# A hybrid decoder step on one core: other numbers in the guess that orders the program

## The chip, the cores and the metric

The kernel runs on one core of a Trainium2 chip. The metric is the device time of one execution in microseconds (us), as the median of several runs. Engines are named as in the profile: PE is TensorE, DVE is VectorE, ACT is ScalarE, POOL is GpSimd, SP is the engine that issues most DMAs.

## The reference

One layer of a causal decoder is computed for a prompt of 2048 tokens and for 8 x 4 sample tokens, all in fp32:

```python
def decoder_layer(x, mk, mv, s5_re, s5_im, ret_s, pos0, p):
    h = rmsnorm(x, p['g_mix'])
    proj = h @ p['w_in']              # columns: u, q, k, v, g
    ...
    ssm_out, s5_re_new, s5_im_new = s5_mixer(...)      # B u, scan over time, C x + D u, gelu, glu
    ret_out, ret_new = retention_mixer(q, k, v, g, ret_s, pos0, p['ret_gn'])  # 4 heads, chunks of 128
    x = x + jnp.concatenate([ssm_out, ret_out], axis=-1) @ p['w_out']
    x = x + memory_attend(rmsnorm(x, p['g_xattn']), mk, mv, p['w_mq'], p['w_mo'])
    h = rmsnorm(x, p['g_mlp'])
    x = x + jnp.square(jax.nn.relu(h @ p['w_up'])) @ p['w_down']
    return x, s5_re_new, s5_im_new, ret_new
```

The width is 1024, the S5 mixer has 512 channels with a complex state, the retention 4 heads of 128, the memory 256 tokens, the MLP 4096 columns. A last RMSNorm follows.

## The kernel before

The prompt is cut into four blocks of 512 tokens (block 1 also carries the 32 sample tokens). Every large product is made of three matmul passes over a high and a low part of each operand. A weight unit of 128x1024 is loaded as `raw`, its high part is taken on ACT and its low part (`whl<-raw,whl`) on DVE as one instruction or on POOL as four.

The program has two halves. The mixer half goes through the blocks: v projection, then for each of the four heads q, k and g, then the u projection of the block; in front of the u projection of blocks 1 to 3 stand the two `w_glu` units of the block before (`dn<-z,whl`, those of block 3 come later). The memory keys and values follow. The second half goes through the blocks again: attention over the memory, MLP, final norm.

The order of all instructions is made when the program is built, and is fixed then. `Order.run` writes the main line: the big matmuls (`dn`, `sc`, `zps`, `tms`), in a sequence that no number changes. Beside it run side chains, generators such as `retention` (one per head and block: `pkd`, `psc`, then `pkv`, then `po`, then `pt`), `ret_sample` (`px`, `po2`, `pn`, `pt2`, which the listings show as `po` and `pt` too), `s5_setup` (`qt`, `km`), `s5_batch` (four per block: `pu`, `vr` and `vi`, then the scan on DVE, then `py`, `pf`, in the sample block also `pvs`, `pys`, `pfs`) and `s5_gelu`. A side chain gives up control at each `yield`, and `Order.poll` resumes it when `od.clock` has come to its wake time. That time is a guess: `Model` keeps when each engine will be free and when each tile is ready, from a fixed and a per-element time for each engine (`RATE`), and adds an offset in ns from the hand-tuned table `SET` (`"sb4": 700`, `"re5": 550`). `od.clock` itself goes on by the guessed time of each matmul (`mm`, `tr`). `Model` also decides which of DVE and POOL takes an operation whose key in `SET` is 2.

At some places the main line may not go on without a chain. `Order.join` then resumes side chains until that chain is done, and writes all that they still have to do into the program before the next main matmul:

```python
def join(self, s):
    self.until(lambda: s.done)

def until(self, cond):
    while not cond():
        self.resume(min(self.sides, key=lambda x: x.wake))
```

The mixer half has four such places that matter here: the end of block 0, where `s5_setup` must be done, and the `w_glu` units of blocks 0, 1 and 2, which stand at the end of the heads of blocks 1, 2 and 3 and wait for the whole S5 chain of the block before, the gelu of its fourth batch included. They are called join 1 to join 4 below. At run time each engine takes its own instructions strictly in the written order and waits on semaphores for the others.

Of the kernel before, what the change touches and what calls it, by code (L numbers as in the profile page):

```python
# [15 lines left out]
PSUM = bass.MemoryType.PSUM  # L16
# [43 lines left out]
class Item:  # L60


    def __init__(self, fn, src=None, eng=None, side=None, cond=None, tight=False, tag="lo"):
        self.fn, self.src, self.eng, self.side, self.cond, self.tight = fn, src, eng, side, cond, tight
        self.raw = self.hl = self.lo = self.again = self.into = None
        self.tag = tag
        self.keep = False
# [7 lines left out]
class Model:  # L75


    RATE = {"V": (65.0, 1.042), "A": (80.0, 0.834), "G": (140.0, 2.11)}

    def __init__(self):  # L80
        self.free = dict(V=0.0, A=0.0, G=0.0, SP=0.0, DMA=0.0)
        self.bufs, self.rings, self.last, self.table = {}, {}, 0.0, None

    def name(self, tile, ring, bufs):
        self.bufs[tile.name] = dict(w={}, r={}, prev=None, ring=(self.rings.setdefault(ring, []), bufs))
        return tile
# [75 lines left out]
    def done(self, eng, name, outs, ins, func=None):  # L162
        n = 1
        for d in max((ap.shape for ap in outs + ins), key=lambda x: len(x) and np.prod(x[1:]))[1:]:
            n *= d
        if name == "dma_start":
            t = self.free["SP"] = max(self.free["SP"] + 60.0, self.after("DMA", outs, ins) - 1200.0)
            t = max(t + 1200.0, self.free["DMA"])
            end = t + 91.0 + 4.0 * n * outs[0].shape[0] / 360.0
            self.free["DMA"] = end  # L170
            self.note("DMA", outs, ins, end)
            return
        c, r = self.RATE[eng]
        end = max(self.free[eng], self.after(eng, outs, ins)) + c + r * n
        if func in (AF.Tanh, AF.Sin, AF.Exp) and func != self.table:
            self.table = func
            end += 1280.0
        self.free[eng] = end
        self.last = max(self.last, end)
        self.note(eng, outs, ins, end)  # L180
# [20 lines left out]
class Either:  # L201
# [5 lines left out]
    def __getattr__(self, name):  # L207
        def call(*args, **kw):
            i = SET[self.key]
            if i == 2:  # L210
# [4 lines left out]
                for e in self.engines:  # L215
                    c, r = Model.RATE[e.key]
                    when.append(max(self.model.free[e.key], self.model.after(e.key, [out], ins, True)) + c + r * n)
# [111 lines left out]
def tile_decoder_step(ctx: ExitStack, tc: tile.TileContext, ins: dict, outs: dict):  # L329
    nc = tc.nc  # L330
    model = Model()
    V, A, G, SY = (Engine(model, e, k) for e, k in ((nc.vector, "V"), (nc.scalar, "A"), (nc.gpsimd, "G"), (nc.sync, "SP")))
# [90 lines left out]
    def split_unit(raw, eng, pool=None, tag="whl", bufs=NW):  # L423
# [4 lines left out]
        def lo():  # L428
            e = eng or min((V, G), key=lambda e: max(model.free[e.key], model.ready(hl)) + 1024 * Model.RATE[e.key][1])
            n = 256 if e is G else 1024  # L430
            for i in range(0, 1024, n):
                e.tensor_tensor(out=hl[:, 1, i:i + n], in0=raw[:, i:i + n], in1=hl[:, 0, i:i + n].bitcast(F32), op=ALU.subtract)
        return hl, lo

    od = Order(model, load_unit, split_unit)

    def mm(out, lhsT, rhs, start, stop):
        n = 1
        for d in rhs.shape[1:]:
            n *= d  # L440
        m = lhsT.shape[1]
        if lhsT.dtype == F32R:
            c = max(0.4217 * n, 107.0 if m > 64 else 56.0)
        else:
            c = max(1.69 * n, 214.0)
        od.work(out, [lhsT, rhs], c)
        T.matmul(out, lhsT, rhs, start=start, stop=stop)  # L447

    def tr(out, in_, idn):
        od.work(out, [in_, idn], 109.0)  # L450
        T.transpose(out, in_, idn)  # L451

    def split_first(dst, src, scale=None):
# [31 lines left out]
    def fm(w, acts, t, out, nk=KT, order=None):  # L485

        for o, n in pieces(t) if isinstance(t, int) else t:
            out.append((dense(), o, n))
        for j, k in enumerate(order or range(nk)):
            for i, (a, b) in enumerate(PASSES):  # L490
                for ps, o, n in out:
                    mm(ps[:, :n], w(k, a), acts[k][:, b, o:o + n],
                       start=(j == 0 and i == 0), stop=(j == nk - 1 and i == 2))
            if j < nk - 1:
                yield

    def stats(pool, acc, cols, eps_tag):

        n = len(cols)
        st = aux("st")  # L500
        ms = pool.tile([P, n], F32, tag=eps_tag + "ms", name="ms")
        full = [i for i, c in enumerate(cols) if c[1] == P]
        part = [i for i, c in enumerate(cols) if c[1] < P]
        for i, (sl, r, *rest) in enumerate(cols):
            for j, s in enumerate([sl] + rest):
                mm(st[:r, 2 * i:2 * i + 2], s, ones, start=(j == 0), stop=(j == len(rest)))
        if part:
            V.memset(ms, 1.0)
        nf = len(full)
        V.tensor_scalar(ms[:, :nf], st[:, 0:2 * nf:2], 1.0 / D, EPS, op0=ALU.mult, op1=ALU.add)  # L510
        for i in part:
            r = cols[i][1]
            V.tensor_scalar(ms[:r, i:i + 1], st[:r, 2 * i:2 * i + 1], 1.0 / D, EPS, op0=ALU.mult, op1=ALU.add)
        return rsqrt(pool, eps_tag, ms, n)
# [5 lines left out]
    def spread(dst, rs, t, last=None, row=None):  # L520

        nt = min(t, BT) // P
        b = aux("sp")
        if row is not None:
            W = [8, 4, P]
            parts = com.tile([P, 2, 4], F32R, tag="parts", name="parts")
            V.tensor_copy(parts[:, 0], rs[:, :4])
            V.tensor_tensor(out=parts[:, 1], in0=rs[:, :4], in1=parts[:, 0].bitcast(F32), op=ALU.subtract)
            yield "sa1"
            tr(b[:8, :P], parts.bitcast(F32).rearrange("p a b -> p (a b)"), ident)  # L530
            r = row[:8, :BT].bitcast(F32R)
            V.tensor_tensor(out=r.rearrange("p (a b) -> p a b", a=4), in0=b[:8, :P].unsqueeze(1).to_broadcast(W),
                            in1=pick.unsqueeze(2).to_broadcast(W), op=ALU.mult)
            yield "sa2"
            mm(b, ones_r.to_broadcast([8, P]), r, start=True, stop=True)
        else:
            for i in range(nt):
                mm(b[:, i * P:(i + 1) * P], rs[:, i:i + 1].to_broadcast([P, P]), ident, start=True, stop=True)
        A.activation(dst[:, :nt * P], b[:, :nt * P], AF.Copy)
        if t > BT:  # L540
            b2 = aux("sp2")
            mm(b2[:, :NS], rs[:NS, last:last + 1].to_broadcast([NS, P]), ident[:NS, :NS], start=True, stop=True)
            A.activation(dst[:, BT:BT + NS], b2[:, :NS], AF.Copy)
        return b
# [338 lines left out]
    def fm_item(src, view, acts, t, done, nk=KT, eng=None, order=None, tag="lo"):  # L883

        def fn(hl):
            for i, w in enumerate(view(hl)):
                out = []
                yield from fm(w, acts() if callable(acts) else acts, t, out, nk, order)
                done(i, out)
                yield  # L890
        return Item(fn, src, eng, tag=tag)
# [47 lines left out]
    def mem_items():  # L939
# [10 lines left out]
        def kv(which, o):  # L950
            def done(i, out):
                ps = out[0][0]

                def ev():
                    od.join(M["ld"])
                    sg = mk((P, TM_), "wst")[:, :MEM]
                    V.tensor_tensor(out=sg, in0=ps[:, :MEM], in1=M["rb"], op=ALU.mult)
                    SY.dma_start(outs[f"m{which}T"][o], sg)
                    t = mk((P, 2, MEM), f"{which}t").bitcast(F32R)
                    split_first(t, sg)  # L960
                    split_rest(t, sg)
                    T_[which].append(t)
                M.setdefault("ev", []).append(ev)
                if which == "v" or o:
                    for e in M["ev"]:
                        e()
                    M["ev"].clear()
            return fm_item(ins[f"w_m{which}"][o], one, acts, MEM, done, eng=ve(f"e_m{which}1" if o % 2 else f"e_m{which}"), tag="l_m" + which)
# [274 lines left out]
    def s5_chain(B):  # L1243
# [21 lines left out]
        def u4_of(be):  # L1265
            pu = aux2("pu")
            for j in range(4):
                tr(pu[:, j * P:(j + 1) * P], uT[:, 4 * be + j].rearrange("p a b -> p (a b)"), ident)
            u4 = mb((P, 4, P), "u4", 2)
            A.activation(u4, pu.rearrange("p (a b) -> p a b", a=4), AF.Copy)  # L1270
            mats["u4"] = u4
            B["u_read"] = be == 3
# [1102 lines left out]
```

## Time and profile before

| what | value |
|---|---|
| time, median of 3 runs | 3056.98 us (3055.93 to 3063.95) |
| the profiled execution | 3057.99 us, its span 3055.8 us |
| PE busy | 2944.5 us, 96% |
| DVE busy | 1767.3 us, 58% |
| POOL busy | 1314.5 us, 43% |
| ACT busy | 1007.1 us, 33% |

The span is the time from the first to the last instruction; the rest of the execution's time lies around it. PE is the engine whose idle time counts. Blocks 0 to 3 of the mixer half lie between about 30 and 756 us of the span, the second half from 968 us on. Idle time of the other engines costs nothing by itself.

### The profile page before, as it was taken

Reading aid. Unit: us, or ns where it says so; the run is one execution under the profiler, and the core shown is the slowest. Engines: PE = TensorE matmul, PEld = TensorE weight load, DVE = VectorE, ACT = ScalarE, POOL = GpSimd, SP = SyncE. Lnnn points to the kernel's source line nnn. Section 1 sums busy time; section 2 is a strip of 40 time slices with the busy share of each in tenths; the row PEclk is TensorE's granted clock in tenths of the full one; section 3 lists DMA queues with packets and bytes.
Section 4 is the critical chain, followed back from the end, with each engine's and each line's share of the span. In section 5 each row is a group of like instructions: output and inputs, shape, how many; then the busy total and the mean of one; then the engine's idle time right before and its main releaser. Section 6 shows DMA issues by size and latency. Waiting matters only on the chain.

```text
span 3055.8 us, 43238 instructions
## 1 busy us (share of the span) xinstructions
PE 2944.5 (96%) x16676; PEld 2561.3 (84%) x16676; DVE 1767.3 (58%) x3088; ACT 1007.1 (33%) x1440; POOL 1314.5 (43%) x1463
## 2 busy tenths in 40 slices
PE   8898899998989999999999999999999999999998
PEld 6688788877987978888987888788999998978887
DVE  8968858779675654334465555556533444553334
ACT  4442232322454332223333333433322223432222
POOL 5534434344565153334534344462433326153334
PEclk9999999999999999999999999999999999999999
DMA  5453253342685222234324444542222233232222
GB/s 151 137 171 111 83 154 119 115 156 75 230 269 168 90 93 95 96 97 141 114 88 145 145 149 148 198 134 83 91 84 90 90 132 122 81 99 94 96 90 76
DMA packets 138957, 374.37 MB, mean 123 GB/s; under 512 B 18656, under 2 KB 39808, under 8 KB 138752
## 3 DMA queue, kind: packets, MB, share of 16 engines
q1 hardware_dynamic: 138176, 371.10, 37.3%
q8 instruction: 131, 2.15, 0.3%
q14 instruction: 74, 0.61, 0.1%
q10 hardware_dynamic: 576, 0.52, 0.1%
HBM read 334.17 MB, written 37.40 MB: 122 GB/s over the span
## 4 chain that ended last, share of the span: by engine, by line
PE 65%; DVE 1%; issue 0%; DMA 0%; ACT 0%; POOL 0%; POOLq 0%; SPq 0%; ACTq 0%; DVEq 0%
PE dn L447 57%; PE sc L447 6%; PE zps L447 1%; DVE rst L197 1%; PE ptp L451 0%; PE st L447 0%; DVE rsy L197 0%; DMA raw<-in_w_down 0%; DVE act L197 0%; PE sp L447 0%; POOL x L197 0%; DVE mx L197 0%; ACT x L197 0%; DVE stage L197 0%; DVE ms L197 0%
## 5 line engine op out<-in xcount | busy, mean ns | idle before, releaser
L447 PE MATMUL dn<-actl,whl 128*128 128x512 f32 (+2 forms) x4656 | 916.3, 356 | 2.2 <-DVE x L197 2.2
L447 PE MATMUL dn<-act,whl 128*128 128x512 f32 (+2 forms) x4704 | 913.3, 348 | 2.1 <-POOL whl L197 1.6
L197 POOL TENSOR_TENSOR whl<-raw,whl 128x256 fp32r<-128x256 f32 x896 | 692.7, 805 | 510.8 <-ACT whl L197 494.3
L447 PEld LDWEIGHTS dn<-actl,whl 128*128 128x128 f32 x4656 | 767.7, 188 | 130.5 <-ACT whl L197 1.9
L447 PEld LDWEIGHTS dn<-act,whl 128*128 128x128 f32 x4704 | 752.7, 189 | 110.8 <-issue 3.0
L197 ACT ACTIVATE whl<-raw 128x1024 fp32r<-128x1024 f32 (+1 forms) x505 | 523.2, 1046 | 650.7 <-PE dn L447 460.5
L197 DVE TENSOR_TENSOR x<-dn,x 128x512 f32<-128x512 f32 (+2 forms) x496 | 291.4, 606 | 430.7 <-PE dn L447 430.2
L197 DVE TENSOR_TENSOR whl<-raw,whl 128x1024 fp32r<-128x1024 f32 (+1 forms) x281 | 400.0, 1429 | 174.3 <-ACT whl L197 164.2
L447 PE MATMUL dn<-z,whl 128*128 128x512 f32 (+1 forms) x2160 | 435.1, 352 | 0.0
L447 PEld LDWEIGHTS dn<-z,whl 128*128 128x128 f32 x2160 | 353.4, 188 | 56.5 <-issue 1.1
L197 POOL TENSOR_TENSOR actl<-sq,actl 128x512 fp32r<-128x512 f32 (+1 forms) x128 | 171.2, 1338 | 455.0 <-DVE sq L197 445.4
L197 DVE SCALAR_TENSOR_TENSOR relu<-dn,rb 128x512 f32<-128x512 f32 (+1 forms) x160 | 91.6, 589 | 323.4 <-PE dn L447 316.0
L197 ACT ACTIVATE actl<-relu 128x512 fp32r<-128x512 f32 (+1 forms) x128 | 82.2, 642 | 512.5 <-DVE relu L197 512.5
L447 PE MATMUL dn<-whl,act 128*128 128x512 f32 x768 | 203.0, 413 | 11.6 <-ACT whl L197 6.3
L197 POOL TENSOR_TENSOR acc<-acc,relu 128x512 f32<-128x512 f32 (+2 forms) x77 | 107.4, 1394 | 237.1 <-ACT relu L197 235.0
L447 PEld LDWEIGHTS dn<-whl,act 128*128 128x128 f32 x768 | 168.0, 255 | 35.9 <-ACT whl L197 7.0
L197 DVE TENSOR_TENSOR sq<-relu 128x512 f32<-128x512 f32 (+1 forms) x128 | 91.6, 715 | 14.8 <-POOL actl L197 2.3
L447 PE MATMUL sc<-whl,act 128*128 128x256 f32 x576 | 80.3, 291 | 14.2 <-ACT p L197 9.4
L447 PEld LDWEIGHTS sc<-whl,act 128*128 128x128 f32 x576 | 75.1, 197 | 15.6 <-ACT p L197 10.0
L447 PE MATMUL sc<-whl,z 128*128 128x256 f32 x576 | 80.8, 291 | 0.0
L197 DVE SCALAR_TENSOR_TENSOR act<-x,small,act 128x512 fp32r<-128x512 f32 (+2 forms) x76 | 64.4, 854 | 28.2 <-ACT act L197 28.2
L197 ACT ACTIVATE act<-x,small 128x512 fp32r<-128x512 f32 (+2 forms) x76 | 53.0, 701 | 72.8 <-DVE x L197 52.9
(318 smaller groups left out, 2671.8 us busy)
## 6 DMA issues: line engine op xcount, KB each, us to landing
raw<-in_w_up SPq DMA_DIRECT2D x128, 512.0 KB, 3.5
raw<-in_w_down SPq DMA_DIRECT2D x128, 512.0 KB, 3.5
raw<-in_w_out SPq DMA_DIRECT2D x32, 512.0 KB, 3.5
raw<-wq_d SPq DMA_DIRECT2D x32, 512.0 KB, 3.5
raw<-wo_d SPq DMA_DIRECT2D x32, 512.0 KB, 3.5
x<-in_xT SPq DMA_DIRECT2D x48, 256.0 KB, 4.3
pm<-pm_d SPq DMA_DIRECT2D x16, 768.0 KB, 5.3
tab<-tab_d SPq DMA_DIRECT2D x16, 516.0 KB, 4.4
```

The lines of the kernel that those rows point to most:

```text
L197: return f(*args, **kw)
L447: T.matmul(out, lhsT, rhs, start=start, stop=stop)
```

## The change

The guess gets other numbers: larger fixed times for DVE, ACT and POOL instructions and slightly larger times per element, larger times for matmuls (230 instead of 216 ns for one of 512 columns), and a new rule: an instruction of DVE with two inputs that both lie in SBUF, if it would start within one of the last 64 POOL instructions, starts when that instruction ends. Nothing else is touched, the table `SET` neither.

```diff
-    RATE = {"V": (65.0, 1.042), "A": (80.0, 0.834), "G": (140.0, 2.11)}
+    RATE = {"V": (146.0, 1.046), "A": (183.0, 0.852), "G": (185.0, 2.16)}
...
+        self.held = deque(maxlen=64)
...
-        end = max(self.free[eng], self.after(eng, outs, ins)) + c + r * n
+        start = max(self.free[eng], self.after(eng, outs, ins))
+        if eng == "V" and name in ("tensor_tensor", "scalar_tensor_tensor") and all(x.space != PSUM for x in ins):
+
+            for lo, hi in self.held:
+                if lo <= start < hi:
+                    start = hi
+        end = start + c + r * n
+        if eng == "G":
+            self.held.append((start, end))
...
-            c = max(0.4217 * n, 107.0 if m > 64 else 56.0)
+            c = max(0.422 * n + 14.0, 111.0 if m > 64 else 60.0)
         else:
-            c = max(1.69 * n, 214.0)
+            c = max(1.69 * n + 14.0, 222.0)
...
-        od.work(out, [in_, idn], 109.0)
+        od.work(out, [in_, idn], 113.0)
```

What it does to the order is seen in the written program. The two programs hold the same PE instructions (15861 matmuls and transposes). DVE has 3061 instructions instead of 3090, POOL 1533 instead of 1468; among what went from DVE to POOL are 12 weight units (12 instructions less on DVE, 48 more on POOL).

**Join 3, on PE** (the `w_glu` units of block 1, behind head 3 of block 2). `dn<-act,whl` is the main line before the join, `dn<-z,whl` the main line behind it; the rest are side chains. Before:

```order
L447 MATMUL dn<-act,whl 128x512 x6
L451 MATMUL pfs<-ident,yT 128x8 x4
L447 MATMUL dn<-act,whl 128x512 x36
L451 MATMUL pkd<-ident,kr 128x128 x4
L447 MATMUL psc<-qr,kr 128x128 x4
L447 MATMUL dn<-act,whl 128x512 x6
L447 MATMUL pkv<-tm_4232,kd 128x128 x4
L447 MATMUL dn<-z,whl 128x272 x12
```

The last piece of block 1's S5 chain on PE (`pfs`) has 42 main matmuls behind it before the join. With the change the last main matmuls before the join and the first ones behind it read:

```order
L460 MATMUL pt<-ident,scs 128x128 x4
L456 MATMUL dn<-act,whl 128x512 x27
L460 MATMUL pkd<-ident,kr 128x128 x4
L456 MATMUL psc<-qr,kr 128x128 x4
L456 MATMUL py<-pm_4871,u_4656 128x128
L456 MATMUL py<-pm_4871,t_5084 128x128
L456 MATMUL py<-pm_4871,t_5085 128x128
```

```order
L460 MATMUL pfs<-ident,yT 128x8 x4
L456 MATMUL vr<-u_5082,q_5222 128x128 x4
L456 MATMUL vi<-u_5082,q_5222 128x128 x4
L460 MATMUL pt<-ident,scs 128x128 x4
L456 MATMUL py<-pm_5254,u_5082 128x128
L456 MATMUL py<-pm_5254,t_5349 128x128
L456 MATMUL py<-pm_5254,t_5350 128x128
```

The 27 `dn` are the last main matmuls before the join. Between them and `dn<-z,whl` stand, with no main matmul among them, the end of the third S5 batch of block 1 (`py` in the first listing), the retention of block 2's head 3, the whole fourth batch (from `vr` in the second listing to `pf`, `pys` and another `pfs`), and then 96 `dn<-z,whl` in one piece.

**Join 4, on PE** (the `w_glu` units of block 2, behind head 3 of block 3). Before:

```order
L447 MATMUL dn<-act,whl 128x512 x6
L451 MATMUL pf<-ident,yT 128x128 x4
L447 MATMUL dn<-act,whl 128x512 x6
L451 MATMUL pt<-ident,scs 128x128 x4
L447 MATMUL dn<-act,whl 128x512 x24
L451 MATMUL pkd<-ident,kr 128x128 x4
L447 MATMUL psc<-qr,kr 128x128 x4
L447 MATMUL dn<-act,whl 128x512 x3
L447 MATMUL dn<-z,whl 128x512 x3
```

With the change:

```order
L456 MATMUL vi<-u_6656,q_6438 128x128 x4
L456 MATMUL dn<-act,whl 128x512 x30
L460 MATMUL pt<-ident,scs 128x128 x4
L460 MATMUL pkd<-ident,kr 128x128 x4
L456 MATMUL psc<-qr,kr 128x128 x4
L456 MATMUL pkv<-tm_5981,kd 128x128 x4
L456 MATMUL po<-tm_5981,scs 128x128
L456 MATMUL po<-S_106,qr 128x128
```

The 39 main matmuls that stood between the last S5 piece (`pf`) and the join are gone: behind the 30 `dn` come two heads' ends (`pt`, then `pkd` to another `pt`), then `py` and `pf` of the fourth batch, and directly `dn<-z,whl` 48 times.

**Join 3, on DVE**, what stands between the `po` of head 3 and the fourth batch's `py`. `t_5293`, `t_5294`, `t_5349`, `t_5350` are the batch's work tiles, `Yr` and `Yi` its scans, `yT` and `z` the gelu of the third batch:

```order
L206 TENSOR_SCALAR scs<-po,mv,rsy 128x128 x4
L206 TENSOR_TENSOR t_5294<-vi,tab 128x4x128
L206 COPY Yr<-carr 128x4
L206 COPY Yi<-cari 128x4
L206 SCALAR_TENSOR_TENSOR yT<-yT,yS 128x544
L206 TENSOR_TENSOR z<-yT,z 128x544
L206 SCALAR_TENSOR_TENSOR stage<-pt,gnh,gate 128x512
L206 SCALAR_TENSOR_TENSOR Yr<-rho_86,carr,t_5293 128x128 x4
L206 SCALAR_TENSOR_TENSOR Yi<-rho_86,cari,t_5294 128x128 x4
L206 TENSOR_TENSOR t_5349<-Yr,tab 128x516
L206 TENSOR_TENSOR t_5350<-Yr,tab 128x516
L206 TENSOR_TENSOR t_5349<-t_5349,gl 128x516
```

and then `t_5350<-t_5350,Yi`. Before, the same stretch of the fourth batch stood in the heads of block 2, where `Sv`, `gate`, `bs` and `mv` of a head lie between its rows and PE has main matmuls to do meanwhile:

```order
L197 TENSOR_TENSOR t_5111<-Yr,tab 128x516
L197 TENSOR_TENSOR whl<-raw,whl 128x1024
L197 SCALAR_TENSOR_TENSOR gate<-gth,gate 128x512
L197 SCALAR_TENSOR_TENSOR S_104<-Sv,pkv 128x128
L197 BN_STATS bs<-po 128x6 x4
L197 BN_AGGR mv<-bs 128x2 x4
L197 TENSOR_TENSOR t_5110<-t_5110,gl 128x516
```

What moved is the fourth batch's scan and what follows it: from among the main matmuls to a place with none.

## Rows read from the trace of the kernel before

**Rows 1.** The page's head and part 1: busy us, share, instructions.

```profile
span 3055.8 us, 43238 instructions
...
PE 2944.5 (96%) x16676; PEld 2561.3 (84%) x16676; DVE 1767.3 (58%) x3088; ACT 1007.1 (33%) x1440; POOL 1314.5 (43%) x1463
```

**Rows 2.** Windows, blocks 0 to 3: length, busy PE, PEld, DVE, ACT, POOL, clock, DMA.

```profile
60.00:190.00 130.00, 117.18 (x603) 99.42 (x601) 115.59 (x236) 55.99 (x82) 63.48 (x63) 0.95 0.46 155
190.00:355.00 165.00, 147.76 (x1062) 135.63 (x1062) 131.80 (x318) 40.60 (x60) 80.14 (x95) 0.98 0.35 106
355.00:571.00 216.00, 204.07 (x1160) 171.11 (x1160) 157.68 (x340) 63.41 (x95) 85.36 (x85) 0.99 0.39 121
571.00:756.00 185.00, 169.95 (x934) 149.01 (x933) 148.70 (x283) 58.76 (x89) 77.61 (x72) 0.98 0.41 133
```

**Rows 3.** Waits of PE, 60 to 190 us: total, times, longest.

```profile
PE pt L451 <- DVE scs L197: 10.1, 4, 4.4
```

**Rows 4.** Waits of PE, 190 to 355 us.

```profile
PE pkd L451 <- POOL kr L197: 4.0, 4, 1.4
PE pkv L447 <- DVE scs L197: 3.7, 2, 2.4
```

**Rows 5.** Waits of PE, 355 to 571 us.

```profile
PE py L447 <- DVE t L197: 6.7, 4, 3.2
```

**Rows 6.** Waits of PE, 571 to 756 us.

```profile
PE pkd L451 <- POOL kr L197: 6.2, 4, 2.1
PE py L447 <- DVE t L197: 5.0, 4, 3.2
```

**Rows 7.** Waits of PE in the second half, 968 us to the end.

```profile
PE sp L451 <- DVE parts L197: 4.8, 4, 1.3
```

**Rows 8.** The chain that ended last, a stretch of main matmuls: start, us, what.

```profile
1093.22 349.56 PE dn L447 x1539
```

**Rows 9.** Groups by shape on DVE, 200 to 800 us: count, busy, mean ns.

```profile
L197 DVE TENSOR_TENSOR_SCAN Yi<-rho,cari,t 128x128 f32<-128x128 f32 x45 | 29.6, 714 | 0.0
L197 DVE TENSOR_TENSOR t<-Yr,tab 128x516 f32<-128x516 f32 x24 | 28.2, 1215 | 0.2
L197 DVE TENSOR_TENSOR_SCAN Yr<-rho,carr,t 128x128 f32<-128x128 f32 x44 | 24.2, 609 | 0.0
...
L197 DVE TENSOR_SCALAR scs<-po,mv,rsy 128x128 f32<-128x128 f32 x48 | 16.4, 405 | 0.4
L197 DVE TENSOR_TENSOR t<-vi,tab 128x512 f32<-128x512 f32 x22 | 15.1, 688 | 3.1 <-PE vi L447 1.7 <-POOL t L197 0.8
...
L197 DVE BATCH_NORM_STATS2 bs<-po 128x6 f32<-128x128 f32 x48 | 10.6, 281 | 5.3 <-PE po L447 5.3
```

**Rows 10.** Timeline of DVE, a head's small chain, its first and last instruction.

```profile
513.45 0.22 DVE L197 TENSOR_SCALAR ve<-mv,rvec 128x4 f32<-128x4 f32 x1
...
515.28 0.23 DVE L197 TENSOR_SCALAR rsy<-rsy,rvec 128x4 f32<-128x4 f32 x1
```

**Rows 11.** Timeline, the gelu of block 1's fourth batch, from eviction to tanh.

```profile
559.00 0.20 ACT L197 ACTIVATE yS<-pfs 128x32 f32<-128x32 f32 x1 [0.33 <-PE pfs L451]
559.23 0.66 ACT L197 ACTIVATE yT<-yS 128x544 f32<-128x544 f32 x1
...
561.16 0.66 ACT L197 ACTIVATE yT<-yT 128x544 f32<-128x544 f32 x1 [1.27 <-DVE yT L197]
```

**Rows 12.** Timeline of PE: four fp32 matmuls of 128 columns (two records each).

```profile
754.25 1.06 PE L447 MATMUL psc<-qr,kr 128*128 128x128 f32 x8
```

**Rows 13.** Timeline of POOL, first and last rows of 16 back-to-back instructions.

```profile
661.48 1.77 POOL L197 TENSOR_TENSOR kr<-kr,tmp 128x512 f32<-128x512 f32 x1 [3.47 <-DVE tmp L197]
...
670.12 2.79 POOL L197 TENSOR_TENSOR whl<-raw,whl 128x256 fp32r<-128x256 f32 x4
```

**Rows 14.** Timeline of DVE at the same time.

```profile
661.43 2.37 DVE L197 TENSOR_TENSOR t<-Yr,tab 128x516 f32<-128x516 f32 x2
```

**Rows 15.** Windows around a wait of PE in the second half, columns as in Rows 2.

```profile
1500.00:1502.30 2.30, 0.18 (x2) 0.00 (x0) 2.13 (x9) 0.00 (x0) 2.30 (x8) 1.00 0.53 196
...
1504.00:1506.70 2.70, 2.70 (x14) 2.70 (x14) 1.54 (x3) 1.07 (x3) 0.00 (x0) 0.50 0.09 33
```

## Prediction

> **What bounds the kernel now.** The page comes first: PE is busy 2944.5 of 3055.8 us, so 111 us are all that any order of the instructions can win [rows 1]. Windows by stage show where they lie: in blocks 0 to 3, from 60 to 756 us, PE is idle for 12.8, 17.2, 11.9 and 15.1 us, 57 us together [rows 2]. Most of the remainder lies in the start, the memory part and the ends of stages. DVE is the second engine in these blocks: 115.6 of 130 us in block 0, 73 to 80% in the others. The waits of PE say what it stood for: small waits at the steps of the side chains, 1 to 4 us each, for the retention's `pt` (10.1 us in block 0) [rows 3], its `pkd` and `pkv` [rows 4], the S5 chain's `py` [rows 5], and both in block 3 [rows 6]. The second half has four waits for `parts`, one per block, 4.8 us together [rows 7]. The reader is to see that PE's work is the same in both programs, so the change is worth what it takes off these waits, less the waits that it makes.
>
> **The change, part by part.** Are the new rates nearer to the trace? A main matmul of 512 columns takes 349.56/1539 = 0.227 us [rows 8]; the guess said 0.216 and now says 0.230. A DVE product of 512 elements takes 0.688 us [rows 9]; it said 0.598, now 0.682. So the rates are better, and by themselves they make side chains resume later, which gives PE more main matmuls to do while it would have waited.
>
> The rule for DVE beside POOL is another matter. It compares the start with each stored POOL instruction in turn and moves it to that one's end; where POOL's instructions follow each other without a gap, the start is carried through the whole run. The trace shows such a run: 16 POOL instructions from 661.48 to 672.91 us [rows 13]. Two DVE products with both inputs in SBUF, issued at its start, were through after 2.37 us [rows 14], where two take 1.4 us alone at 0.69 each: they stood for about 1 us, not for the 11 us of the run. So here the rule puts the side chains too late. The Trainium skill ("SBUF — State Buffer", section "Who interferes with whom") says the same of the chip: a DVE instruction with two SBUF inputs and a POOL instruction that reads SBUF exclude each other for the length of one instruction. If the rule of the change were right instead, the chains would not be ready before their new places, the joins would cost nothing extra, and the sum below would end at its gains alone, 3022 us; rows 13 and 14 speak against that.
>
> The order listings show the consequence: the S5 chain of each block no longer ends ahead of its join, and what is left is written there in one piece with no main matmul in it. DVE cannot run ahead, since its queue holds `gate<-dn,rb` of the last main matmuls in front. What PE then waits for is added up from rows.
>
> Join 3. (A) `pt` of head 3 needs, after `po`: four `bs` (4 x 0.281), three products of `vr` and `vi` (3 x 0.688) that stand before the small chain, that chain (513.45 to 515.51, 2.06 [rows 10]) and the first `scs` (0.405): 5.7 us. PE has `pfs`, `vr`, `vi` meanwhile, about 2.1 us at 1.06 per four [rows 12]: wait 3.5. (B) `py` needs one product (0.69), two gelu operations (2 x 0.69, the price of the same width), `stage` (0.69), eight scans (4 x 0.609 + 4 x 0.714 = 5.3), two `t<-Yr` (2.43) and two more products (1.38) [rows 9]: 11.9 us, less 1.4 of `pt` and the first `py`: wait 10.5. (C) Two evictions on ACT between `py`, `pf`, `pys` and `pfs`, 0.6 each: 1.2. (D) The gelu of the fourth batch: 559.00 to 561.82 [rows 11], then DVE, ACT, DVE at 0.69, 0.66, 0.69: 4.9 us, less the 18 `dn<-z` of 272 columns that need only the first three z tiles (18 x 0.227 x 272/512 = 2.2): wait 2.7. Join 3 costs 18 us; before, 42 main matmuls or 9.5 us hid the gelu.
>
> Join 4, by the same rows: `po` waits for `scs`, behind seven DVE operations (5.5 us, less 4.2 for 16 matmuls: 1.3), then for `Sv` behind four scans and a `gate` (3.4 - 0.8 = 2.6), `pt` for four scans, `bs`, two `t<-Yr`, the small chain and `scs` (8.9 - 1.1 = 7.8), `py` 0.4, an eviction 0.6, the gelu 4.9 - 9 x 0.227 = 2.9: together 16 us.
>
> Joins 1 and 2 are shorter. At join 1 the products of the last setup batch remain, some five DVE and POOL operations of 0.7 to 1 us less eight transposes: 3 us. At join 2 `py` and `pf` and two retention steps: 6 us, as (A) and (D) with most of the gelu hidden. Sum of the losses: 18 + 16 + 3 + 6 = 43.
>
> The gains: in block 0 three of the four `pt` get 12 more main matmuls between `po` and `pt` (24 to 36, 33 to 45, 24 to 36), 2.7 us against waits of 1.5 to 2.5; the longest, 4.4, goes from 30 to 27 and stays: 10.1 - 4.4 = 5.7 [rows 3]. In block 1 `pkd` stands 12 to 18 matmuls later: 4.0 + 3.7 [rows 4]. In blocks 2 and 3 the waits at `py` go, either because a batch has 6 to 78 more matmuls or because its place is now in a join: 6.7 [rows 5] and 5.0; `pkd` in block 3 stands 18 to 24 later: 6.2 [rows 6]. `parts` has 6 more in each block, 1.4 us against 1.3 at most: 4.8 [rows 7]. Sum 36.
>
> Two smaller terms. PE's clock: after PE stood idle in 1500 to 1502.3 us, the granted clock of the busy stretch behind it was 0.50, the 1.2 GHz level, where 14 matmuls took the time of 28 [rows 15]. Each of three long waits (B, and two in join 4) should cost 1 to 2 us in that way, and some of the old waits no longer do: net 2. The units that go from DVE to POOL: DVE loses 12 of them, POOL gains 48 quarters. Outside the blocks PE has main matmuls of other units to do, so I take 2 us, between nothing and the 4 us that a few late quarters could cost. For the moves of the sample chain in block 1 to later places I take nothing: between a gain and a loss of 5 us (it has `po2` right behind `px` once, and elsewhere more cover than before).
>
> The sum is 43 + 2 + 2 - 36 = +11 us on the profiled execution's 3057.99, which lies 1 us above the median: 3068 us.
>
> **The rivals.** *No change that can be measured.* A difference under 0.3% (9 us) is about what a measurement of this kernel can't tell from none. If 42 of the 57 us of idle time in the blocks go, instead of the 31 counted, the gains are 47 with `parts` and meet the losses: about 3057. For it: the listings show more cover at nearly every step. Against it: DVE is busy 89% of block 0, so its waits can't all go.
>
> *Faster.* One mechanism: DVE reaches the joins with little left, since waits (B) and the 7.8 of join 4 rest on means that hold POOL collisions (scans of 0.61 to 0.71). With both halved the losses are 34; with 50 won in the blocks that is 16 us faster, 3041. It decides where joins 3 and 4 together cost under 18 us (then the losses are 27, and the gains as counted are 9 more). Against it: the rows of DVE between `vi` and `py` are in strict order, and eight scans and four products can't take less than about 7 us.
>
> *Much slower.* At the joins DVE comes late as well as the chain: POOL has more units, and every DVE operation in (B) can meet one. With each of the 13 operations of (B) and of join 4 waiting 0.7 us more, the losses grow by 18, and new small waits in block 1 eat 5 of the gains: 3091.
>
> *The change doesn't do what it says* is the case weighed above: a guess that is right would place nothing late; 3022.
>
> **How the numbers follow.** Chances: my forecast 0.42, no change 0.28, faster 0.15, much slower 0.12, the right guess 0.03. The forecast lies just above the line of 0.3% (3066), so some of it falls below that line: slower by over 0.3% gets 0.47, within 0.3% 0.34, faster 0.19. The range reaches from the faster case to the much slower one: 3042 to 3093; the forecast's own range is 3055 to 3080.
>
> **What would show it.** Right: in the profile after, PE's waits for `pt`, `pkd` and `py` from 60 to 500 us shrink to less than half; just ahead of the `dn<-z` of blocks 1 and 2, PE has two waits of over 5 us each, ended by DVE's `t` and `scs`, and the clock is 0.5 behind them; the waits for `parts` are gone; PE's busy time stays within a few us of 2944. Wrong: waits at joins 3 and 4 under 10 us together, or small waits in blocks 0 and 1 that are as many as before, or a new large wait in the memory part for `whl` from POOL.

## The result, and the profile after

The changed kernel takes 3129.91 us (median of 4 runs, 3121.66 to 3131.51) against 3057.34 for the kernel before on the same chip: 1.0228 times the time, interval 1.0204 to 1.0251. It is slower by some 70 us; forecast were 11, and the range ended at 3093. The profiled execution took 3130.61 us. The head of its page and part 1, beside [rows 1]:

```profile
span 3128.8 us, 43294 instructions
...
PE 2964.1 (95%) x16676; PEld 2583.9 (83%) x16676; DVE 1779.3 (57%) x3059; ACT 1010.1 (32%) x1442; POOL 1370.4 (44%) x1528
```

PE has the same 16676 matmul records and is busy 19.6 us longer, and its idle time, span less busy, went from 111.3 to 164.7 us. These two differences, 19.6 and 53.4, are the 73.0 us by which the span grew. Windows by stage, cut at the joins as in [rows 2], show where it lies:

```profile
60.00:196.00 136.00, 117.83 (x592) 100.25 (x591) 110.81 (x233) 56.22 (x80) 67.91 (x73) 0.92 0.40 131
196.00:387.00 191.00, 160.30 (x1109) 148.16 (x1109) 143.89 (x332) 45.43 (x66) 84.11 (x101) 0.92 0.35 104
387.00:623.50 236.50, 210.69 (x1155) 178.05 (x1153) 169.33 (x348) 61.38 (x91) 99.64 (x99) 0.92 0.37 111
623.50:833.00 209.50, 177.03 (x941) 155.25 (x940) 152.63 (x277) 58.93 (x89) 84.41 (x84) 0.93 0.35 118
```

The four rows are 77 us longer than those of before, and PE's idle time in them is 107.2 us for 57.0. The granted clock is 0.92 or 0.93 in all four, where it was 0.95 to 0.99. Behind block 3 little is lost: from the first `dn<-z` of block 3 to the end it was 2300 us (755.84 to 3055.8), and is now 2296 (832.99 to 3128.8). The two cuts don't part quite the same work: the end of block 3's head 3 (`pkv`, `po` and `pt`) stood behind the first and stands ahead of the second.

The waits of PE in blocks 0 to 3 (total, times, longest), the largest of each block, beside [rows 3 to 6]:

```profile
PE dn L456 <- DVE gate L206: 4.9, 1, 4.9
PE pt L460 <- DVE scs L206: 4.5, 1, 4.5
PE km L456 <- DVE pm L206: 3.3, 1, 3.3
...
PE pt L460 <- DVE scs L206: 10.6, 2, 6.7
PE po L456 <- DVE s L206: 5.2, 1, 5.2
PE pn L456 <- DVE S L206: 3.5, 1, 3.5
...
PE py L456 <- DVE t L206: 9.8, 1, 9.8
PE pt L460 <- DVE scs L206: 5.9, 1, 5.9
PE pkd L460 <- POOL kr L206: 5.7, 2, 4.5
...
PE pt L460 <- DVE scs L206: 12.9, 2, 7.8
PE py L456 <- POOL t L206: 5.5, 1, 5.5
PE psc L456 <- ACT kd L206: 4.3, 2, 3.5
```

Where before many small waits stood, there are few long ones. Those at the joins are `km` in block 0, one `pt` of 3.9 in block 1, `py` and `pt` in block 2, and `pt` of 7.8 with `psc` in block 3. The rest lies within the blocks, and was not forecast. In the second half the waits for `parts` are still there, against [rows 7]:

```profile
PE sp L460 <- DVE parts L206: 5.5, 4, 1.5
```

### The profile page after: what moved, and what is told of

The parts are those of the page before. It is cut to its first block, busy times and chain, and to the rows that moved or that the text cites. A ratio compares the mean times of both kernels' runs of the same rounds, so it can differ in the third digit from the quotient of the medians.

```text
span 3128.8 us, 43294 instructions
## 1 busy us (share of the span) xinstructions
PE 2964.1 (95%) x16676; PEld 2583.9 (83%) x16676; DVE 1779.3 (57%) x3059; ACT 1010.1 (32%) x1442; POOL 1370.4 (44%) x1528
## 4 chain that ended last, share of the span: by engine, by line
PE 63%; DVE 2%; DMA 0%; issue 0%; ACT 0%; POOL 0%; SPq 0%; POOLq 0%; ACTq 0%; DVEq 0%
PE dn L456 55%; PE sc L456 6%; PE zps L456 1%; DVE rst L206 1%; PE ptp L460 0%; PE st L456 0%; DVE rsy L206 0%; DMA raw<-in_w_mos 0%; DVE whl L206 0%; DMA raw<-in_w_down 0%; SPq L206 0%; PE sp L456 0%; POOL x L206 0%; ACT whl L206 0%; DVE act L206 0%
## 5 line engine op out<-in xcount | busy, mean ns | idle before, releaser
L206 POOL TENSOR_TENSOR whl<-raw,whl 128x256 fp32r<-128x256 f32 x944 | 732.8, 807 | 537.5 <-ACT whl L206 529.5
L206 DVE TENSOR_TENSOR whl<-raw,whl 128x1024 fp32r<-128x1024 f32 (+1 forms) x269 | 389.3, 1453 | 163.9 <-ACT whl L206 154.7
L206 POOL TENSOR_TENSOR t<-t,t 128x512 f32<-128x512 f32 x16 | 20.6, 1286 | 134.7 <-DVE t L206 123.9
```

Source lines behind the costliest of these rows:

```text
L206: return f(*args, **kw)
```

## The experiments

Four theories were put against each other. **A**: side chains resume too late, above all because the rule carries a DVE start through a whole run of POOL instructions, and what is left at the joins stands open. **B**: the offsets of SET were set with the cheap rates, so that dearer rates alone loosen the order. **C**: the units that go from DVE to POOL cost. **D**: any other order than that of before loses, whichever way it moves. All ratios are against the kernel before on the same chip; the last column is what the ratio lies above 1, times 3057 us. Medians of different runs may come from different chips, so the ratios are what is compared.

| run | what is new | us, median | ratio, interval | about |
|---|---|---|---|---|
| e1 | rule alone | 3075.73 | 1.0066, 1.0043 to 1.0088 | +20 |
| e2 | rates alone | 3095.22 | 1.0123, 1.0097 to 1.0149 | +38 |
| e3 | PE costs alone | 3097.93 | 1.0138, 1.0114 to 1.0162 | +42 |
| e4 | all but the rule | 3086.57 | 1.0095, 1.0069 to 1.0121 | +29 |
| e5 | new guess for the order alone | 3115.32 | 1.0188, 1.0165 to 1.0212 | +57 |
| e6 | new guess for DVE or POOL alone | 3070.19 | 1.0042, 1.0028 to 1.0056 | +13 |
| e7 | all, rule cut to one wait | 3094.20 | 1.0115, 1.0094 to 1.0137 | +35 |
| e8 | DVE's fixed cost 75 for 65 ns | 3069.43 | 1.0043, 1.0028 to 1.0057 | +13 |
| e9 | new order in blocks 2 and 3 alone | 3109.73 | 1.0173, 1.0158 to 1.0189 | +53 |
| e10 | new order everywhere else | 3070.19 | 1.0033, 1.0019 to 1.0048 | +10 |
| e11 | full change, joins filled | 3139.45 | 1.0270, 1.0251 to 1.0289 | +83 |
| e12 | new choices in the second half | 3054.54 | 0.9994, 0.9984 to 1.0004 | -2 |
| e13 | full change, three waits filled | 3130.64 | 1.0226, 1.0208 to 1.0244 | +69 |
| e14 | full change again | 3129.99 | 1.0221, 1.0201 to 1.0240 | +68 |

**The parts of the change (e1 to e4, e7).** e1 is the full change with the old RATE and the old PE costs:

```diff
-    RATE = {"V": (146.0, 1.046), "A": (183.0, 0.852), "G": (185.0, 2.16)}
+    RATE = {"V": (65.0, 1.042), "A": (80.0, 0.834), "G": (140.0, 2.11)}
...
-            c = max(0.422 * n + 14.0, 111.0 if m > 64 else 60.0)
+            c = max(0.4217 * n, 107.0 if m > 64 else 56.0)
```

e4 is the full change without the rule, and e2 is e4 with the old PE costs:

```diff
-            for lo, hi in self.held:
-                if lo <= start < hi:
-                    start = hi
```

e3 is the kernel before with the new PE costs:

```diff
-            c = max(0.4217 * n, 107.0 if m > 64 else 56.0)
+            c = max(0.422 * n + 14.0, 111.0 if m > 64 else 60.0)
```

> The old rates and the old guess of PE's costs, with the rule for DVE beside POOL added. Theory A (the rule carries DVE's starts through whole runs of POOL and so puts the side chains too late): this alone brings most of the loss, 3105 to 3130 us, with several us of waits just ahead of the dn<-z of the blocks. Theory B (the dearer rates loosen the order, since the offsets in SET were set for the cheap ones): 3050 to 3070 us. Theory C (POOL gets more units, 1508 POOL instructions here against 1468 before and 1533 after): 3090 to 3100 us, in proportion to the 40 of 65 instructions.

> The new rates of DVE, ACT and POOL alone, no rule and the old guess of PE's costs. Theory A: within 15 us of before, 3045 to 3070 us. Theory B: most of the loss, 3105 to 3130 us; here PE's guess stays at 0.216 us for a main matmul while the other engines get slower, so chains resume at still later main matmuls than in the full change, and it can be as slow as that. Theory C (1516 POOL instructions): 3095 to 3110 us.

> Only the guess of PE's costs is new (a main matmul 0.230 us for 0.216), so that side chains resume some main matmuls earlier; no PE work of a side chain is left at a join, and POOL has 1471 instructions for 1468. Theory A and B: nothing is late at a join, so within 10 us of before; if less cover at each step costs what the small waits of blocks 0 to 3 cost, up to 10 us slower, 3057 to 3070 us. Theory C: as before, 3050 to 3062 us.

> The full change without the rule: new rates and new PE costs. Theory A: the loss is gone, 3040 to 3070 us. Theory B: most of the loss stays, 3100 to 3130 us, since chains still resume after a guess that is longer by 0.08 us for each DVE and 0.10 us for each ACT operation. Theory C (1492 POOL instructions): 3080 to 3090 us.

e7 cuts the loop short:

```diff
             for lo, hi in self.held:
                 if lo <= start < hi:
                     start = hi
+                    break
```

> The full change with the rule cut to one wait: a DVE product waits for the one POOL instruction that runs at its start, and not for those behind it (1517 POOL instructions, 5, 3, 7 and 7 pieces at the joins). Theory A: the rule's share of the loss is gone, so about what the full change without the rule gave, 3075 to 3095 us. Theories C and D: between that and the full change, 3095 to 3125 us.

No theory had all of this. The rule alone costs 20 us and the rates alone 38, so neither A nor B is the whole: A's range was met by e7 alone, B's by none. C's range holds e2 and e4, but not e1 and e3. On top of the rest the rule costs 70 - 29 = 41 us, of which the `break` takes 35 away: the carrying through whole runs is what is dear in it. (The `break` also moves some choices between DVE and POOL: e7 has 1517 POOL instructions for 1533.) One wait (1.0115) and none (1.0095) can't be told apart, their intervals overlap.

e3 was the surprise. With dearer PE costs the chains resume *earlier*, nothing is left at a join, POOL has 3 instructions more, and it is as slow as the rates alone. Waits of PE from 60 to 1000 us, of before and of e3:

```profile
PE pkd L451 <- POOL kr L197: 11.4, 10, 2.1
...
PE dn L447 <- POOL whl L197: 4.4, 6, 0.9
...
PE po L447 <- DVE Sv L197: 2.8, 2, 1.4
```

```profile
PE pkd L451 <- POOL kr L197: 24.8, 12, 5.1
PE dn L447 <- POOL whl L197: 11.2, 12, 3.0
...
PE po L447 <- DVE Sv L197: 11.0, 6, 3.5
```

Chains that come earlier have less main work between their steps, and the steps stand open: 28 us more in these three rows. That is 28 of the 42 us. So the guess loses in both directions from where it stood, and e4, with rates and PE costs that are nearer to the trace than those of before (for a main matmul and a DVE product, as the prediction compared them), still loses 29.

**Order or engine (e5, e6).** Two models run side by side while the program is built; one sets when chains resume, the other serves the choices in `Either` and `lo`.

```diff
-    model = Model()
+    model = Model(True, Model(False))
...
-                    when.append(max(self.model.free[e.key], ...
+                    when.append(max(self.model.other.free[e.key], ...
```

That is e5; e6 has `Model(False, Model(True))`.

> Two guesses run side by side while the program is built: the new one (rates, rule and PE costs) sets when side chains resume, the old one chooses between DVE and POOL. The PE work left at joins 1 to 4 is that of the full change (4, 8, 18 and 8 pieces), POOL has 1481 instructions. Theory A (late chains): nearly the whole loss, 3110 to 3130 us. Theory C (the units that go to POOL): most of the loss is gone, 3060 to 3085 us. Theory D (the offsets in SET fit the order of before alone, and every other order loses some tens of us in new places): slower than before too, 3080 to 3130 us, without saying where.

> The reverse: the old guess sets when side chains resume, the new one chooses between DVE and POOL (1517 POOL instructions, 49 more than before; at most one piece of PE work is left at a join). Theory A: within 10 us of before, 3047 to 3067 us. Theory C: most of the loss, 3100 to 3130 us. Theory D: 3070 to 3100 us, since the choices move work that the offsets were fitted to.

57 for the order and 13 for the choices: together the 70 of the change. In e5 A's and D's ranges were met and C's was not. In e6 D's was met, A's was missed by 3 us, and C, which wanted most of the loss there, got less than a fifth of it. Block by block they don't add up as neatly: between main matmuls 480 and 1176 (block 1) e5 takes 172 us, before 173 and the full change 196; from there to 1728 (block 2) 250, 216 and 236. Where a loss falls depends on both.

**A small push (e8).**

```diff
-    RATE = {"V": (65.0, 1.042), ...
+    RATE = {"V": (75.0, 1.042), ...
```

> Before, with one number moved a little: DVE's fixed cost in the guess 75 ns for 65, an eighth of the change's step. Theories A to C: too small to matter, within 6 us of before, 3050 to 3063 us. Theory D: any other order loses, 10 to 40 us, 3066 to 3097 us.

10 ns on a DVE instruction, an eighth of the step that the change makes, cost 13 us. A to C said nothing of the kind; that is D, at its low end. It is one push of one number; how much others cost was not measured.

**Which blocks (e9, e10).** The order changes from one guess to the other at main matmuls 1176 and 2304; the clocks of the sides are carried over.

```diff
+    SWITCH = (1176, 2304)
...
+            if self.mains - 1 in self.SWITCH:
+                self.guess = 1 - self.guess
+                d = self.models[self.guess].clock - self.clock
...
+                for s in self.sides:
+                    s.wake, s.last = s.wake + d, s.last + d
```

> The new guess sets the order from main matmul 1176 to 2304 alone (blocks 2 and 3, with joins 3 and 4: 18 and 8 pieces of PE work left there); everywhere else, and in every choice between DVE and POOL, the old guess stands. Theory A (the joins): most of what the new order costs in the whole kernel (60 us), 3100 to 3115 us. Theory D (every block loses with any other order): about half of it, 3080 to 3092 us.

> The reverse: the new guess sets the order everywhere but from main matmul 1176 to 2304 (4 and 8 pieces at joins 1 and 2, none at 3 and 4). Theory A: what joins 1 and 2 cost less the waits won in blocks 0 and 1, 3055 to 3068 us. Theory D: the other half, 3080 to 3092 us.

A was right on the place: with the new order in blocks 2 and 3 alone nearly all of e5's loss is there, and without them 10 us remain, no more than e8 (2 us above A's range, 10 below D's). The windows of e9 for blocks 2 and 3, and its largest waits there (block 2, then block 3):

```profile
359.00:602.00 243.00, 215.11 (x1178) 181.59 (x1177) 172.56 (x364) 61.38 (x91) 88.44 (x88) 0.92 0.35 108
602.00:810.00 208.00, 180.47 (x939) 157.63 (x939) 152.11 (x282) 58.86 (x89) 74.46 (x70) 0.92 0.36 118
```

```profile
PE py L477 <- DVE t L213: 12.1, 1, 12.1
PE pt L481 <- DVE scs L213: 9.5, 2, 5.0
...
PE pt L481 <- DVE scs L213: 10.4, 2, 7.8
PE psc L477 <- ACT kd L213: 5.1, 3, 2.4
PE pkd L481 <- POOL kr L213: 4.0, 1, 4.0
```

Against [rows 2] PE is idle 28 us longer in these blocks (55.4 for 27.0) and busy 21.6 us longer, at a clock of 0.92 for 0.98 and 0.99.

**Wait or clock (e11, e13, e14).** The waits at joins 3 and 4 are filled with matmuls whose results are overwritten: 128x512 float32, of constants, into the PSUM tile that the next piece writes.

```diff
         py = aux2("py")
+        cover(py, 9, (1728,))
...
         pt_ = aux("pt")
+        cover(pt_, 6, (1728, 2304))
```

That is e11. In e13 the counts are `11 * (be == 3)` and `7 * (h == 3)`: the fourth batch and head 3 alone.

> The full change, with matmuls that compute nothing of use put ahead of the pieces that wait at joins 3 and 4: 9 into py at join 3 and 6 into pt at joins 3 and 4 (128x512 float32, overwritten by the real ones; some 0.87 us each, so 7.8 us in a wait of 9.8, 5.2 in one of 5.9 and 5.2 in one of 7.8). If the half clock behind the joins comes of PE standing idle, the stages up to joins 3 and 4 lose the half clock: 8 to 14 us less than the full change, 3115 to 3122 us. If the clock has another cause, or the fill itself runs at half clock and makes the real work late: 3128 to 3150 us.

e11 doesn't tell the two apart: its condition also held for the `py` of the third batch and for another `pt`, which had no wait. That is new work on the path, and `vi` of the fourth batch starts 8.1 us later than in the full change (599.58 for 591.44). By the ratios its time lies some 13 us above the full change (+83 for +70). e13 fills the three waits alone, with the full change beside it.

> The full change, with the idle matmuls in the three long waits alone: 7 into the pt of head 3 at joins 3 and 4, 11 into the py of the fourth batch at join 3 (some 0.89 us each; 6.2, 9.8 and 6.2 us into waits of 5.9, 9.8 and 7.8). If the half clock is what the joins cost beyond their waits (PE's busy time in blocks 2 and 3 is 14 us above before): the pieces between py and the first dn<-z of join 3 take about 9.5 us for 13.5, and the whole 8 to 15 us less than the full change beside it. If the DVE chain sets the length of the joins whatever PE's clock: within 4 us of the full change.

> The full change again, as the neighbour of the exact fill: 3122 to 3135 us.

PE at join 3 in the full change, start and us, then in e13:

```profile
598.35 1.43 PE L460 MATMUL pt<-ident,scs 128*128 128x128 f32 x4 [5.85 <-DVE scs L206]
...
610.00 1.40 PE L456 MATMUL py<-pm,t 128*128 128x128 f32 x4 [9.79 <-DVE t L206]
...
611.62 1.06 PE L456 MATMUL py<-pm,t 128*128 128x128 f32 x4
...
623.52 2.54 PE L456 MATMUL dn<-z,whl 128*128 128x272 f32 x18
627.95 0.52 PE L456 MATMUL dn<-z,whl 128*128 128x272 f32 x2 [1.88 <-ACT z L206]
```

```profile
600.55 9.61 PE L462 MATMUL py<-rmask,ident 128*128 128x512 f32 x22
...
611.08 1.10 PE L457 MATMUL py<-pm,t 128*128 128x128 f32 x4 [0.70 <-DVE t L206]
...
612.24 0.61 PE L457 MATMUL py<-pm,t 128*128 128x128 f32 x4
...
620.88 2.54 PE L457 MATMUL dn<-z,whl 128*128 128x272 f32 x18
```

The windows of the same stretches (the clock is the third number from the end), the full change and then e13:

```profile
592.00:610.00 18.00, 2.36 (x12) 1.47 (x10) 16.75 (x35) 1.31 (x2) 8.22 (x6) 0.57 0.13 44
610.00:624.00 14.00, 12.60 (x73) 10.66 (x74) 1.80 (x9) 2.12 (x5) 0.78 (x2) 0.70 0.01 1
```

```profile
593.00:610.00 17.00, 17.00 (x47) 7.65 (x46) 15.75 (x34) 1.31 (x2) 7.78 (x6) 1.00 0.15 46
610.00:621.00 11.00, 8.78 (x74) 7.46 (x73) 2.89 (x10) 1.80 (x4) 1.25 (x3) 1.00 0.01 1
```

The fill holds the clock at 1.00, four `py` matmuls take 0.61 us for 1.06, and from the first `py<-pm,t` to the first `dn<-z` it is 9.8 us for 13.5. So half clock costs 3.7 us at join 3. The waits themselves are as long, filled or not, since DVE sets their end: from `pt` to the first `py<-pm,t` it is 11.65 us in both, and DVE is busy 16.75 of the 18 us of the first window. In the time of the whole run nothing is seen (3130.64 beside 3129.99, with intervals of some 5 us to either side): of the two readings the second, within 4 us, was met, and not the 8 to 15 us. In the profiled executions the stretch with the fill (main matmuls 1176 to 2304) takes 440.3 us in e13 and 445.2 in e14, but ahead of it and behind it, where the two programs are the same, e13 takes 5.6 us more: a gain of this size drowns in the scatter of single executions.

**A try at a better version (e12).**

```diff
+        def cho():
+            return model.other if model.mains >= 3312 else model
...
-            e = eng or min((V, G), key=lambda e: max(model.free[e.key], model.ready(hl)) ...
+            e = eng or min((V, G), key=lambda e: max(cho().free[e.key], cho().ready(hl)) ...
```

> A try at a version that beats both: the old guess throughout, but from main matmul 3312 on (the second half) the new guess chooses between DVE and POOL, 25 more POOL instructions; the order does not move. In the profile of the run that had the new choices everywhere this part took 2073 us for 2081 before. Theory C (more POOL work costs): 3065 to 3080 us. If that profile's 8 us are real: 3045 to 3050 us. If they were the scatter of single executions: 3052 to 3060 us.

No change, so the 8 us in the profile of e6 were the scatter of single executions, as the third reading had it, and 25 units more on POOL cost nothing in that half. No version here beats the kernel before.

## Why the prediction was wrong

**Right: the direction, the place and the joins.** The rule puts chains too late by carrying starts through POOL's runs (35 us by e7), the pieces are left at the joins, and joins 3 and 4 carry the loss (e9). The sums held too, in part by luck. Join 3 was put at 18 us and has 5.9 + 9.8 + 0.7 + 0.7 + 2.1 = 19.2; join 4 at 16, measured 18.1; join 1 at 3, measured 5.1; join 2 at 6, measured 6.4. Together 49 for the 43 forecast. But in join 4 the forecast waits come to 11.8 (its `pt` was worked out at 7.8 and was 7.8; `po` and `Sv` were to be 3.9 and are 0.6), and `pkd` and `psc`, 6.3 together, were not in the sum. In join 3 the eight scans of (B) took 3.2 us, not 5.3 (the mean that priced them holds slow ones), and slower products and a wait for ACT made up for it; (A) was 5.9 for 3.5. The Trainium skill ("SBUF — State Buffer", section "Who interferes with whom") has the two engines exclude each other for an instruction; the rows of DVE and POOL at join 3 agree: a DVE product of 1.19 us ends 0.02 us behind POOL's instruction, where its neighbour takes 0.16. In the guess, one wait (+35 us in all) costs far less than the run of them (+70), but no wait at all (+29) can't be told from one.

**Failed: "The gains: ... Sum 36".** This is the step that broke. Blocks 0 to 3 have 107.2 us of idle time; less the 46 of the joins that fall into these windows, 61 remain, for 57.0 before [rows 2]. They were to be 26 (57 less 31). The old waits did become fewer, as forecast: `pt` in block 0 stands once for 4.5, not four times for 10.1; in block 1 `pkv` stands for 1.1 and `pkd` not at all, where they had 3.7 and 4.0. But others took their places: `dn<-gate` 4.9 and `psc` in block 0, `pt` 6.7, `po` 5.2 and `pn` 6.0 in block 1, `py` behind POOL's `t` 5.5 and `pt` 5.1 in block 3. I counted each step's cover by its main matmuls and let DVE's queue behind it stay as it was. Of the signs named beforehand, the nearest to this is "small waits in blocks 0 and 1 that are as many as before": they are fewer, but PE's idle time there is 48.9 us for 30.0. Of the signs of being right only the two long waits of join 3 came in full; the waits for `parts`, 4.8 of the 36, stayed at 5.5. The windows of three of the new waits (`po`, `pt`, `py`; columns as in [rows 2]):

```profile
297.31:302.54 5.23, 0.00 (x0) 0.00 (x1) 5.09 (x8) 0.00 (x0) 4.04 (x4) 0.85 0.00 0
356.94:363.69 6.75, 0.00 (x2) 0.00 (x1) 6.41 (x19) 0.00 (x0) 3.21 (x4) 0.65 0.00 0
695.95:701.43 5.48, 0.00 (x0) 0.00 (x0) 1.58 (x1) 0.00 (x0) 5.48 (x7) 0.59 0.54 192
```

In the first two DVE is busy 95 to 97% of the time, and in the other new waits behind DVE 93 to 100%: its queue sets their end. In the third it is POOL's queue, and DVE is mostly idle.

One price in the prediction was too low for this. The small chain that each head has ahead of `scs` was taken at 2.06 us [rows 10], from a place where POOL was busy for only 0.33 us. In blocks 1 to 3 the twelve such chains took 27.2 us together before and take 44.6 with the change, up to 6.5 each, since more of them now stand beside POOL's instructions. At join 3 the chain takes 4.11 us; its first, slowest and last row, and the POOL instruction beside the slowest:

```profile
593.74 0.92 DVE L206 TENSOR_SCALAR ve<-mv,rvec 128x4 f32<-128x4 f32 x1
...
595.61 1.19 DVE L206 SCALAR_TENSOR_TENSOR rsy<-rst,rsy 128x4 f32<-128x4 f32 x1
...
597.62 0.23 DVE L206 TENSOR_SCALAR rsy<-rsy,rvec 128x4 f32<-128x4 f32 x1
```

```profile
595.45 1.33 POOL L206 TENSOR_TENSOR yT<-yT,yS 128x544 f32<-128x544 f32 x1
```

The next instruction of the same shape takes 0.16 us; this one ends with POOL's, 0.02 us behind it. The 2.05 us above the price are most of what (A) lacked, and the `pt` of 5.1 in block 3 has a chain of 5.9 ahead of it. It isn't the whole of the loss: in e3 the twelve chains take 31.7 us and in e8 26.6, and both are slower than before. No run took these collisions away alone.

In blocks 2 and 3 with the order alone (e9), some 17 of 55.4 us lie outside the joins, for 27.0: there 10 of the 18 us did come.

**Failed in size: "PE's clock ... net 2".** PE's busy time rose by 19.6 us (22 in e9). At the long wait of join 3, half clock costs 3.7 us by e13, and about 1 at join 4, by how much that stage of e13 is shorter. So of the three long waits that were to cost 1 to 2 us each, one cost twice that and the other two together less; the rest, some 15 us, is spread over the four blocks, all at 0.92 or 0.93, and no run takes it apart. One more stretch can be read off: from 359.0 to 372.6 us, around the `pt` of 6.7, the clock was 0.50 and PE busy 8.1 us, so half of that, some 4 us, is the clock's price there, as an estimate. The Trainium skill ("TensorE: Matmul & The Clock Gate", section "Terms") prices a lowered clock at its time multiplied by the share of pulses that is lost. The mean clocks of 0.988 and 0.974 over the spans make 73 and 163 us at half clock, so by that an estimate of 45 us more; PE's busy time shows less than half of it, and that measurement decides: PE stood idle in much of that time (in the window from 592 us it was busy 2.36 of 18 us at 0.57).

**Failed in size: the units that go to POOL, 2 us.** e6 has 13. But e8 costs 13 without any such purpose, so this may be the price of any other order, and no run tells the two apart. Outside the blocks, where the prediction expected little, e12 shows no cost.

**Failed: "by themselves they make side chains resume later, which gives PE more main matmuls to do".** The rates without the rule cost 29 to 38 us, the PE costs alone 42; the rival *the right guess* (3022) rested on the same belief. Here a guess nearer to the trace wasn't worth more.

In sum: joins 49, waits elsewhere in blocks 0 to 3 up by 4, PE's busy time 20: 73, for 72.6 us between the two profiled executions. The forecast had 43, -34 (the gains less 2 for the units) and 2. So of the 62 us that it was short, 38 are waits elsewhere, 18 are PE's busy time and 6 the joins.

Left open: whether offsets in SET set anew for the new guess would win the loss back. That they fit the old guess is what e3, e4 and e8 point to, all slower in different directions; a new setting wasn't tried, so this is argued and not shown.

## What to carry to other kernels

A table of guessed times that sets an order, and offsets tuned beside it, are best taken as one object: correcting the table alone moves steps everywhere, and here ten nanoseconds in one entry already cost 13 us. Whoever forecasts such a change should count joins (work that has to be done before the next stage, priced by the engine that feeds it; in sum that came out within 6 of 43 us), but credit no gain from wider cover unless the queue of the engine behind it is followed too, with prices from places that are as crowded as the new ones. A push of one entry by a small step gives, for one run, a first size of what a reordering can cost; measure it before sizing the rest.

## What was not expected of the hardware

Behind a short wait after full-speed work PE's clock fell in one place and not in another. In e11 the granted clock was 1.00 through the fill and a wait of 2.41 us, and 0.50 from 619.46 to 622.00 us behind it; `py` matmuls took 1.06 us for four:

```profile
607.62 7.89 PE L462 MATMUL py<-rmask,ident 128*128 128x512 f32 x18
...
618.14 1.10 PE L457 MATMUL py<-pm,t 128*128 128x128 f32 x4 [2.41 <-DVE t L206]
...
619.46 1.06 PE L457 MATMUL py<-pm,t 128*128 128x128 f32 x4
```

Before the change, through a wait of 3.17 us and behind it, the clock was 1.00, and the same four took 0.61 us:

```profile
548.29 0.71 PE L447 MATMUL py<-pm,t 128*128 128x128 f32 x4 [3.17 <-DVE t L197]
...
549.06 0.61 PE L447 MATMUL py<-pm,t 128*128 128x128 f32 x4
```

So the length of a wait alone doesn't tell whether the work behind it runs at half clock, and a count of waits does not price the clock.
